# Other start addresses in on-chip memory for the operands of a decoder block's matrix products

## The chip, the cores and the metric

The kernel runs on one core of one Trainium2 chip. A core has a matrix engine (TensorE; the profile calls its products PE and its weight loads PEld), a vector engine (DVE), a scalar engine (ACT), GpSimd (POOL) and a queue that issues transfers (SP). They share an on-chip memory of 128 partitions; a tile lies at the same byte address in each partition. The metric is the device time of one execution in microseconds (us). Before the change three runs gave 1021.38, 1021.69 and 1025.06 us; the median is 1021.69 us.

## The reference

One decoder layer on 512 tokens of width 1024, all in 32-bit floats:

```python
u = modulate(rmsnorm(h, g_norm_ffn1[l]), sh1, sc1)
h = h + 0.5 * gt1 * swiglu(u, w_ffn1_in[l], w_ffn1_out[l])
u = modulate(rmsnorm(h, g_norm_mix[l]), sh2, sc2)
h = h + gt2 * token_mixing(u, cos, sin, w_in[l], ...)
u = modulate(rmsnorm(h, g_norm_ffn2[l]), sh3, sc3)
h = h + 0.5 * gt3 * swiglu(u, w_ffn2_in[l], w_ffn2_out[l])
return rmsnorm(h, g_final)
```

`swiglu` multiplies u (512 by 1024) with a 1024 by 5632 matrix, combines the halves as silu(a) * b, and multiplies by a 2816 by 1024 matrix. `token_mixing` projects u to 4608 columns, runs a causal pooling mixer and a dilated window attention over parts of them, gates both and projects back to 1024. The nine vectors of shift, scale and gate come from a 1024 by 9216 product with the condition vector.

## The kernel before, in words

**Split operands.** Every large product uses the 4-byte type float32r, and every operand is held as a rounded part ("hi") and a remainder ("lo"). One product is three matmuls (`mm3`, L323 to L325): hi weights with hi activations, hi weights with lo activations, lo weights with hi activations. In each, 128 by 128 weights are loaded into the array (the stationary operand) and the activations stream past them (the moving operand), 512 or 256 columns of tokens at a time. The trace has a weight load for every matmul, and it runs while the matmul before it streams.

**The ring of weights.** Weights come from memory in chunks, mostly 1024 columns wide (4096 bytes per partition), through three raw buffers. ACT writes the hi part into `whi` (L280), DVE the lo part into `wlo` (L292). Both are rings of `RING` = 7168 columns, that is seven chunks; `plan` lists all chunks in the order of use, and `room` (L235) gives each chunk the next place in the ring, in units of 128 columns (256 or 512 for three kinds of chunk in the mixing). A unit that does not fit before the end of the ring starts again at its beginning, so a chunk may be written in two pieces, which is one more instruction on ACT and one more on DVE. The splitting runs three or four chunks ahead of TensorE.

**Activations.** `UH` and `UL` hold u of the current sub-layer (eight tiles of 512 tokens), `HI` and `HK` the hi and lo parts of silu(a) * b, `MH` and `ML` those of the gated merge, `SH0..2` and `SL0..2` three sums of blocks of u.

**Three kinds of rows of products.** (1) Products with 512 columns: the first pairs of an FFN (`ffn_pair`; in the first FFN four pairs at once in `startup`, L1482 to L1486), the tiles of the mixing, and the output products of the FFN on `HI`/`HK`. (2) `duo` (L714): two pairs of an FFN's hidden tiles as seven block products in place of eight, each one chunk and 24 matmuls of 256 columns (`product`, L703; matmuls at L710, L711, L712). The fourth sum is a part of u itself; product 2 of a duo uses the sum `SH0`/`SL0`, product 3 `S1`, product 5 `S2`, the four others u. There are 16 duos, in eight rows; between two rows stand four chunks of output products (96 matmuls of 512 columns). (3) The ends of the three sub-layers and the beginning of the next (`out_tail`, `out_end`, `head`): products done first for tokens 0 to 255 and then for 256 to 511, so with 256 columns. Four of the mixing's value products also stream 256 columns, with the roles of weights and u exchanged (L1209 to L1211).

**Where the operands lie.** The tiles are laid out one after the other from address 1152, so that their start modulo 256 bytes is fixed by the sizes of those before. A tile of 128, 256 or 512 columns takes a multiple of 512 bytes, so all matmuls on one tile see the same remainder. In the built program:

| operand | before: start modulo 256 bytes |
|---|---|
| all weights in `whi` and `wlo` | 128 |
| `UH`, `UL` in both FFNs | 64 |
| `UH`, `UL` in the mixing (`place_u` moves them by 16 columns) | 128 |
| sum 0 | 128 |
| sums 1 and 2 (a pad of 192 bytes, `padb`, stands in front) | 64 |
| `HI`, `HK`, `MH`, `ML` and the other operands of the mixing | 128 |

TensorE works through its instructions in the order written; nothing is scheduled automatically.

Of the kernel before, what the change touches and what calls it, by code (L numbers as in the profile page):

```python
# [8 lines left out]
F32 = mybir.dt.float32  # L9
F32R = mybir.dt.float32r  # L10
# [4 lines left out]
P = 128  # L15
T = 512
HT = 256
D = 1024
KT = 8
# [91 lines left out]


FIRST = 4
RING = 7 * 1024


U_AT = (0, 16, 0)

PLAIN = {0: 8, 2: 4}
PARTS = ((0, 4), (4, 8), (8, 12), (12, 16), (16, 22))  # L120
# [3 lines left out]
def pairs_before(n, part):  # L124

    k1 = PARTS[part][1]
    return k1 if part + 1 == len(PARTS) or (n == 2 and part == 0) else k1 + 2


def chunk_widths():  # L130
    outs = [D] * (KT // 2 * (len(PARTS) - 1)) + [(FT - PARTS[-1][0]) * P] * KT
    f1 = [2 * FIRST * P] * KT + [D] * (2 * (FT - FIRST)), outs
    mix = [D] * 20 + [D, D] + [D, D, 4 * P] * (KT - 1) + [4 * P] + [D] * KT
    return f1, mix, ([D] * (2 * FT), outs)


class Kernel:
# [6 lines left out]
    def plan(self):  # L144
        (i1, o1), mix, (i2, o2) = chunk_widths()
        self.chunks = []
        for name, ws in (("wf1i", i1), ("wf1o", o1), ("wmix", mix), ("wf2i", i2), ("wf2o", o2)):
            off, rec = 0, []
            for w in ws:
                rec.append((name, off, w))  # L150
                off += P * w
            self.chunks.append(rec)
        f1i, f1o, mx, f2i, f2o = self.chunks


        self.loads, self.order, self.last = [], [], {}

        def plain(recs):
            for r in recs:
                n = len(self.loads)  # L160
                self.loads.append(r)
                self.last[n] = len(self.order)
                self.order.append((r[2], n, ("raw", n), None))

        def blocks(recs):
            n = len(self.loads)
            self.loads.extend(recs)
            r11, r12, r22, r21 = (("raw", n + i) for i in range(4))
            x0, x1 = ("x", 0), ("x", 1)
            for need, src, make in ((0, r11, None), (1, x0, (x0, r12, r11)), (2, x1, (x1, r22, x0)), (3, r21, None),  # L170
                                    (3, r12, (r12, r22, r12)), (3, r22, None), (3, x0, (x0, r21, x1))):
                for j, x in enumerate((r11, r12, r22, r21)):
                    if x == src or (make and x in make):
                        self.last[n + j] = len(self.order)
                self.order.append((D, n + need, src, make))

        def ffn(n, ins, outs, first):
            j, at = first, 0
            if first:
                plain(ins[:KT])  # L180
                at = KT
            for part, (k0, k1) in enumerate(PARTS):
                while j < pairs_before(n, part):
                    if j < PLAIN[n]:
                        plain(ins[at:at + 2])
                        j, at = j + 1, at + 2
                    else:
                        blocks(ins[at:at + 4])
                        j, at = j + 2, at + 4
                plain(outs[part * KT // 2:(part + 1) * KT // 2] if part + 1 < len(PARTS) else outs[-KT:])  # L190

        ffn(0, f1i, f1o, FIRST)
        base = len(self.order)
        plain(mx)
        ffn(2, f2i, f2o, 0)
        self.fetched = self.done = self.made = 0
        self.pos, self.held, self.retired, self.half = 0, None, [], None
        self.at, self.start, self.top = {}, {}, 0
        self.buf = {}
        self.units = {base + i: 2 * P for i in (4, 5)}  # L200
        self.units.update({base + i: T for i in range(16, 20)})
# [33 lines left out]
    def room(self, i, held):  # L235


        w, u, at, pieces = self.order[i][0], self.unit(i), self.top, []
        for c in range(0, w, u):
            if at % RING + u > RING:  # L240
                at += RING - at % RING
            o = at % RING
            if pieces and pieces[-1][0] + pieces[-1][1].stop - pieces[-1][1].start == o:
                pieces[-1] = (pieces[-1][0], slice(pieces[-1][1].start, c + u))
            else:
                pieces.append((o, slice(c, c + u)))
            at += u
        low = min((self.start[j] for j in range(held, i)), default=self.top)
        return (pieces, at) if at - low <= RING else None

# [201 lines left out]
        self.nc.vector.scalar_tensor_tensor(self.UL[k][:, hs], t[:, hs], S, self.UH[k][:, hs],  # L452
                                            op0=OP.add, op1=OP.subtract)

    def place_u(self, n):
        self.UHv, self.ULv = (x[:, U_AT[n]:U_AT[n] + KT * T] for x in (self.UHall, self.ULall))
        self.UH, self.UL = ([x[:, k * T:(k + 1) * T] for k in range(KT)] for x in (self.UHv, self.ULv))

    def norm_steps(self, n, hs):

        t, done = {}, [0]

        def upto(k):
            while done[0] <= min(k, KT - 1):
                i = done[0]
                if i == 0:
                    t[0] = self.norm_a(n, 0, hs)
                if i + 1 < KT:
                    t[i + 1] = self.norm_a(n, i + 1, hs)
                self.norm_b(n, i, hs, t.pop(i))  # L470
                done[0] += 1
        return upto
# [9 lines left out]
    def out_tail(self, ms, ksrc, gate, nxt, squares):  # L482


        nc = self.nc
        tiles, starts = {}, {}
        A, Bh = slice(0, HT), slice(HT, T)
        step = None
        self.held = self.pos
        for h, hs in enumerate((A, Bh)):  # L490
            for m in ms:
                bank = self.nb()
                if h == 0:
                    starts[m] = self.pos
                    tiles[m] = ksrc(m)
                    starts[m + 1] = self.pos
                if h == 0 and m == ms[0]:
                    nc.scalar.preload_act_table(AF.Sqrt)
                if self.done < self.pos + 4:
                    self.split_hi()  # L500
                ks = tiles[m]
                for i, (hi, lo, uh, ul) in enumerate(ks):
                    if h == 1 and m == ms[1] and i == 3:
                        self.stats_t(self.B[6], A)
                    if h == 1 and m == ms[2] and i == 1:
                        self.spread(self.B[6], A)
                        self.place_u(nxt)
                        step = self.norm_steps(nxt, A)
                        step(0)
                    self.mm3(bank[:, hs], hi, lo, uh[:, hs], ul[:, hs], i == 0, i == len(ks) - 1)  # L510
                s = squares(m)[:, :HT]
                self.tail_step(m, hs, bank, gate, s)
                if h == 1:
                    self.held = starts[m + 1]
                    if step:
                        step(1 if m != ms[-1] else 3)
                self.split_lo()
                nc.vector.tensor_tensor(self.acc[:, hs], self.acc[:, hs], s, op=OP.add)
                self.fetch()
        self.stepA = step  # L520
# [171 lines left out]
    def step(self):  # L692

        self.now += 1
        due = [f for t, f in self.put if t <= self.now]
        self.put = [x for x in self.put if x[0] > self.now]
        for f in due:
            f()
# [105 lines left out]
    def open_sums(self):  # L804
        st = ExitStack()
        bp = st.enter_context(self.tc.tile_pool(name="fs", bufs=1))
        self.S = []
        for i in range(3):
            self.S.append([bp.tile([P, 4 * HT], F32R, name=f"S{x}{i}") for x in "HL"])
            if i == 0:  # L810
                bp.tile([P, 48], F32, name="padb")
        self.S.append([x.rearrange("p (k t) -> p k t", k=KT)[:, :4, HT:] for x in (self.UHv, self.ULv)])
        return st

# [520 lines left out]
    def build(self):  # L1335
# [6 lines left out]
        tl = lambda n, w, dt=F32: per.tile([P, w], dt, name=n)  # L1342
        self.free = [tl(f"raw{i}", CW) for i in range(3)]

        self.hi, self.lo = tl("whi", RING, F32R), tl("wlo", RING, F32R)
        self.vecs = tl("vecs", 106)
        self.H = [tl(f"H{k}", T) for k in range(KT)]
        self.UHall = tl("UH", KT * T + 16, F32R)
        cst, self.eps = tl("cst", 163), tl("eps", 1)
        self.ULall = tl("UL", KT * T + 16, F32R)  # L1350
        self.place_u(0)
        self.AR = tl("AR", 2 * T)
        self.acc, self.R = self.AR[:, :T], self.AR[:, T:]
        self.mod, self.part = tl("mod", 72), tl("part", 1)
# [197 lines left out]
```

## Time and profile before

| | |
|---|---|
| median of the three runs | 1021.69 us |
| the profiled execution: its own time / its span | 1025.08 / 1023.3 us |
| PE busy, matmul records | 1012.1 us, 6364 |
| PEld busy | 914.9 us |
| DVE / ACT / POOL busy | 753.2 / 434.8 / 26.0 us |
| granted TensorE clock over the span | 0.998 |

A matmul's row has a start and a duration. Durations overlap, because the next matmul starts before the last results of the one before are out; what a matmul costs is the distance from its start to the next start. The prediction calls this the pitch, and reads it from the view of instructions in order of time, over a stretch of equal matmuls: time between two starts, divided by the matmuls between them.

### The profile page before, as it was taken

What the parts mean: (1) busy time and instruction counts of PE and PEld (TensorE: products, weight loads), DVE (VectorE), ACT (ScalarE), POOL (GpSimd) and SP (SyncE); (2) the same over time, 40 slices, a digit from 0 to 9 for tenths busy, and PEclk for the clock granted to TensorE, in tenths of its full rate; (3) what the DMA queues carried; (4) which work ended last, traced back from release to release, by engine and by line L of the source; (5) the groups of instructions that cost most, each with busy time, mean ns of one, the idle gap of its engine ahead of it and who ended that gap; (6) DMA issues with size and microseconds to landing.
All of it is one profiled execution on the core that took longest, in us unless ns stands there. A gap on an engine that the chain in (4) does not pass through costs nothing.

```text
span 1023.3 us, 15508 instructions
## 1 busy us (share of the span) xinstructions
PE 1012.1 (99%) x6364; PEld 914.9 (89%) x6364; DVE 753.2 (74%) x1082; ACT 434.8 (42%) x638; POOL 26.0 (3%) x30
## 2 busy tenths in 40 slices
PE   8999999999999999999999999999999999999997
PEld 7888898989999899889988888998899899998997
DVE  6969879889786777779446776577787776676754
ACT  5453352534445552334314333454365354352552
POOL 0000000000000000006100000000000000000001
PEclk9999999999999999999999999999999999999999
DMA  8856365555533513222154774322244234241312
GB/s 315 285 177 256 112 238 162 172 162 188 165 115 106 157 35 103 62 83 83 32 185 156 268 263 127 104 63 72 94 155 135 83 103 145 84 144 45 112 32 83
DMA packets 43113, 139.60 MB, mean 136 GB/s; under 512 B 4897, under 2 KB 8225, under 8 KB 43042
## 3 DMA queue, kind: packets, MB, share of 16 engines
q1 hardware_dynamic: 42354, 137.95, 41.3%
q8 instruction: 50, 0.82, 0.3%
q10 hardware_dynamic: 688, 0.66, 0.2%
q14 instruction: 21, 0.17, 0.1%
HBM read 135.82 MB, written 2.77 MB: 135 GB/s over the span
## 4 chain that ended last, share of the span: by engine, by line
PE 95%; DVE 3%; DMA 1%; ACT 0%; issue 0%; DVEq 0%; ACTq 0%
PE bank L323 17%; PE bank L324 17%; PE bank L325 17%; PE bank L710 10%; PE bank L712 10%; PE bank L711 10%; PE bank L1486 1%; PE bank L1484 1%; PE bank L1482 1%; PE bank L1080 1%; PE bank L1259 1%; PE bank L1411 1%; PE bank L1260 1%; PE bank L1261 1%; PE bank L1028 1%; PE bank L1057 1%
## 5 line engine op out<-in xcount | busy, mean ns | idle before, releaser
L292 DVE TENSOR_TENSOR wlo<-raw,whi 128x1024 fp32r<-128x1024 f32 (+2 forms) x151 | 175.5, 1165 | 69.0 <-ACT whi L280 68.8
L280 ACT ACTIVATE whi<-raw 128x1024 fp32r<-128x1024 f32 (+2 forms) x151 | 150.4, 1003 | 42.6 <-DVE raw L228 39.8
L323 PE MATMUL bank<-UH,whi 128*128 128x512 f32 (+1 forms) x432 | 159.0, 368 | 0.0
L324 PE MATMUL bank<-UL,whi 128*128 128x512 f32 (+1 forms) x432 | 154.9, 359 | 0.2 <-DVE UL L452 0.2
L325 PE MATMUL bank<-UH,wlo 128*128 128x512 f32 (+1 forms) x432 | 154.9, 359 | 0.0
L323 PE MATMUL bank<-HI,whi 128*128 128x512 f32 (+1 forms) x406 | 146.8, 362 | 0.0
L324 PE MATMUL bank<-HK,whi 128*128 128x512 f32 (+1 forms) x406 | 146.5, 361 | 0.0
L325 PE MATMUL bank<-HI,wlo 128*128 128x512 f32 (+1 forms) x406 | 146.5, 361 | 0.0
L710 PE MATMUL bank<-UH,whi 128*128 128x256 f32 x512 | 141.6, 277 | 0.0
L711 PE MATMUL bank<-UL,whi 128*128 128x256 f32 x512 | 141.6, 277 | 0.0
L712 PE MATMUL bank<-UH,wlo 128*128 128x256 f32 x512 | 141.6, 277 | 0.0
L292 DVE TENSOR_TENSOR wlo<-X,whi 128x1024 fp32r<-128x1024 f32 (+2 forms) x88 | 104.4, 1188 | 39.5 <-ACT whi L280 39.3
L710 PE MATMUL bank<-SH,whi 128*128 128x256 f32 x384 | 107.1, 279 | 0.3 <-ACT u L717 0.3
L711 PE MATMUL bank<-SL,whi 128*128 128x256 f32 x384 | 106.9, 278 | 0.0
L712 PE MATMUL bank<-SH,wlo 128*128 128x256 f32 x384 | 106.9, 278 | 0.0
L280 ACT ACTIVATE whi<-X 128x1024 fp32r<-128x1024 f32 (+2 forms) x88 | 89.3, 1028 | 33.1 <-DVE X L228 32.1
L711 PEld LDWEIGHTS bank<-UL,whi 128*128 128x128 f32 x512 | 96.1, 188 | 0.3
L710 PEld LDWEIGHTS bank<-UH,whi 128*128 128x128 f32 x512 | 96.1, 188 | 0.3
L712 PEld LDWEIGHTS bank<-UH,wlo 128*128 128x128 f32 x512 | 96.4, 188 | 0.0
L325 PEld LDWEIGHTS bank<-UH,wlo 128*128 128x128 f32 x432 | 81.3, 188 | 12.8
L324 PEld LDWEIGHTS bank<-UL,whi 128*128 128x128 f32 x432 | 81.5, 189 | 12.3 <-issue 0.5
L323 PEld LDWEIGHTS bank<-UH,whi 128*128 128x128 f32 x432 | 81.4, 189 | 11.9 <-issue 0.5
(225 smaller groups left out, 1748.5 us busy)
## 6 DMA issues: line engine op xcount, KB each, us to landing
ada<-wada SPq DMA_DIRECT2D x47, 512.0 KB, 5.0
raw<-wmix SPq DMA_DIRECT2D x44, 512.0 KB, 3.9
raw<-wf1i SPq DMA_DIRECT2D x34, 512.0 KB, 4.5
raw<-wf2i SPq DMA_DIRECT2D x30, 512.0 KB, 3.6
X<-wf2i SPq DMA_DIRECT2D x14, 512.0 KB, 3.5
cs<-wada SPq DMA_DIRECT2D x12, 512.0 KB, 3.5
AR<-wada SPq DMA_DIRECT2D x12, 512.0 KB, 3.9
raw<-wf2o SPq DMA_DIRECT2D x12, 512.0 KB, 3.6
```

The costliest lines, as they stand in the source:

```text
L280: self.nc.scalar.activation(self.hi[:, y], r[:, x], AF.Copy)
L292: self.nc.vector.tensor_tensor(self.lo[:, y], r[:, x], self.hi[:, y], op=OP.subtract)
L323: M(ps, hi, uh, start=start, stop=False)
L324: M(ps, hi, ul, start=False, stop=False)
L325: M(ps, lo, uh, start=False, stop=stop)
L710: M(o, hi, uh, start=start and p == 0 and k == 0, stop=False, skip_group_check=True)
L711: M(o, hi, ul, start=False, stop=False, skip_group_check=True)
L712: M(o, lo, uh, start=False, stop=k == 3, skip_group_check=True)
L1028: M(S[:, o + i * P:o + i * P + P], qz[:, (2 * i + h) * P:(2 * i + h + 1) * P], k[:, toks], start=True, stop=True)
L1057: nc.tensor.transpose(b[:, i * P:i * P + P], p[:, i * P:i * P + P], self.ident)
L1080: M(o, pt[:, blk * P:blk * P + P], v, start=i == 0, stop=i == len(srcs) - 1)
L1259: M(b, self.UH[k][:, c::4], hi, start=k == 0, stop=False)
```

## The change

`UH` and `UL` get a pad of 16 columns (64 bytes) in front and a fixed place; `place_u` and the pad `padb` go. u and all sums then start at 128 modulo 256 bytes in all sub-layers. A chunk of weights may be marked as shifted: it then starts at 16 columns after a multiple of 64 columns in the ring, which is 192 modulo 256 bytes; others stay at 128. Marked are the chunks of all 256-column products on u, sums, `HI` and `MH` (not the value products with exchanged roles), and the one chunk of 512-column products in front of each row of such chunks. The ring grows from 7168 to 7296 columns. All tiles behind it move by 1024 bytes, which leaves their remainder as it was.

```diff
-RING = 7 * 1024
-U_AT = (0, 16, 0)
+RING = 7 * 1024 + 128
+SHIFT = 16
...
     def blocks(recs):
         n = len(self.loads)
+        self.shifted.update(range(len(self.order) - 1, len(self.order) + 7))
...
+    def shift(i):
+        self.shifted.update(range(len(self.order) - i, len(self.order)))
...
                     if j < PLAIN[n]:
                         plain(ins[at:at + 2])
+                        if n and j < 2:
+                            shift(2)
...
         ffn(0, f1i, f1o, FIRST)
+        shift(5)
         base = len(self.order)
         plain(mx)
+        self.shifted.update(range(base, base + 4))
+        shift(4)
         ffn(2, f2i, f2o, 0)
+        shift(6)
...
         w, u, at, pieces = self.order[i][0], self.unit(i), self.top, []
+        shift = SHIFT if i in self.shifted else 0
+        at += (shift - at) % 64
         for c in range(0, w, u):
             if at % RING + u > RING:
-                at += RING - at % RING
+                at += RING - at % RING + shift
...
-    def place_u(self, n):
-        self.UHv, self.ULv = (x[:, U_AT[n]:U_AT[n] + KT * T] for x in (self.UHall, self.ULall))
...
-            if i == 0:
-                bp.tile([P, 48], F32, name="padb")
...
-        self.UHall = tl("UH", KT * T + 16, F32R)
+        tl("pad0", 16)
+        self.UHv = tl("UH", KT * T, F32R)
         cst, self.eps = tl("cst", 163), tl("eps", 1)
-        self.ULall = tl("UL", KT * T + 16, F32R)
-        self.place_u(0)
+        tl("pad1", 16)
+        self.ULv = tl("UL", KT * T, F32R)
```

In the built programs the instructions of every engine stand in the same order before and after, except that 30 more chunks are written to the ring in two pieces: 30 more instructions at L280 on ACT and 30 more at L292 on DVE. The float32r matmuls by the remainders of weights (w) and moving operand (u):

| columns | before | after | matmuls |
|---|---|---|---|
| 256 | w 128, u 64 | w 192, u 128 | 2496 |
| 256 | w 128, u 128 | w 192, u 128 | 1044 (384 of them on sum 0) |
| 512 | w 128, u 64 | w 128, u 128 | 456 |
| 512 | w 128, u 128 | w 192, u 128 | 228 (chunks in front of rows) |
| 512 | w 128, u 64 | w 192, u 128 | 24 (chunk in front of the first row) |
| 512 | w 128, u 128 | unchanged | 1530 |
| both | value products with exchanged roles | unchanged | 168 |

More of the change, by code (lines that the diff above doesn't have):

```diff
@@ L156, in plan @@
         self.loads, self.order, self.last = [], [], {}
+        self.shifted = set()
         def plain(recs):
@@ L453, in norm_b @@
                                             op0=OP.add, op1=OP.subtract)
-    def place_u(self, n):
-        self.UHv, self.ULv = (x[:, U_AT[n]:U_AT[n] + KT * T] for x in (self.UHall, self.ULall))
-        self.UH, self.UL = ([x[:, k * T:(k + 1) * T] for k in range(KT)] for x in (self.UHv, self.ULv))
     def norm_steps(self, n, hs):
@@ L506, in out_tail @@
                         self.spread(self.B[6], A)
-                        self.place_u(nxt)
                         step = self.norm_steps(nxt, A)
@@ L1347, in build @@
         self.H = [tl(f"H{k}", T) for k in range(KT)]
-        self.UHall = tl("UH", KT * T + 16, F32R)
+        tl("pad0", 16)
+        self.UHv = tl("UH", KT * T, F32R)
         cst, self.eps = tl("cst", 163), tl("eps", 1)
-        self.ULall = tl("UL", KT * T + 16, F32R)
-        self.place_u(0)
+        tl("pad1", 16)
+        self.ULv = tl("UL", KT * T, F32R)
+        self.UH, self.UL = ([x[:, k * T:(k + 1) * T] for k in range(KT)] for x in (self.UHv, self.ULv))
         self.AR = tl("AR", 2 * T)
```

## The prediction

> **What bounds the kernel now.** I read the page first (busy times, then the chain that ended last, then the costliest groups), and after it TensorE's instructions in order of time, where the starts show what one matmul costs. The first fence is the page.
>
> ```profile
> PE 1012.1 (99%) x6364; PEld 914.9 (89%) x6364; DVE 753.2 (74%) x1082; ACT 434.8 (42%) x638; POOL 26.0 (3%) x30
> PE 95%; DVE 3%; DMA 1%; ACT 0%; issue 0%; DVEq 0%; ACTq 0%
> L710 PE MATMUL bank<-UH,whi 128*128 128x256 f32 x512 | 141.6, 277 | 0.0
> ```
>
> TensorE is busy 99% of the span and carries 95% of the chain; the large groups have no idle time before them (last column). In the view of waits TensorE waits 3.3 us in the start-up and 1.1 us in four places after it. So nothing but the pitch of the matmuls sets the end, and a pitch changed by p ns on n matmuls moves the end by n times p.
>
> The next fence is the view in order of time (start in us, duration, engine, line). It holds the first row of five stretches of equal matmuls, and each time the row that follows the stretch.
>
> ```profile
> 108.87 0.39 PE L323 MATMUL bank<-UH,whi 128*128 128x512 f32 x1
> ...
> 131.27 0.28 PE L710 MATMUL bank<-UH,whi 128*128 128x256 f32 x1
> ...
> 134.00 0.28 PE L710 MATMUL bank<-SH,whi 128*128 128x256 f32 x1
> ...
> 136.86 0.29 PE L710 MATMUL bank<-SH,whi 128*128 128x256 f32 x1
> ...
> 150.48 0.39 PE L323 MATMUL bank<-HI,whi 128*128 128x512 f32 x1
> ...
> 172.26 0.28 PE L710 MATMUL bank<-UH,whi 128*128 128x256 f32 x1
> ...
> 175.09 0.28 PE L710 MATMUL bank<-SH,whi 128*128 128x256 f32 x1
> ...
> 177.96 0.29 PE L710 MATMUL bank<-SH,whi 128*128 128x256 f32 x1
> ```
>
> All weights start at 128, so only the moving operand differs. Pitches:
> - 512 columns, u at 64 (108.87 to 131.27, four chunks of 24): 22.40 us / 96 = 233.3 ns.
> - 512 columns, `HI` at 128 (150.48 to 172.26): 21.78 / 96 = 226.9 ns.
> - 256 columns, u and sums 1, 2 at 64 (136.86 to 150.48, five products): 13.62 / 120 = 113.5 ns; single matmuls alternate 113, 113, 114, so 113.3 settled.
> - 256 columns, sum 0 at 128 (134.00 to 136.86 and 175.09 to 177.96): 119.2 and 119.6 ns. The 256-column ends on `HI` and `MH` at 128 run at 119.9 in the same view.
> - 256 columns, u at 64, but right behind a row of 512 columns at 128 (172.26 to 175.09): 2.83 / 24 = 117.9 ns, to the end of the product. Behind a row of 512 columns at 64 (131.27 to 134.00) it is 113.8. So there are two settled pitches at the same addresses, and what ran before picks one.
>
> The start address is thus worth 6.4 ns a matmul, with opposite signs: 512 columns want 128 against 128, 256 columns want 64 bytes between weights and u.
>
> **The change part by part.** It goes by the profiled execution, 1025.08 us (span 1023.3), 3.4 us above the median of the runs; each saving is taken off the median too.
>
> (1) *512-column products on u in the FFNs go to 128/128*: 456 matmuls from 233.3 to 226.9: 456 x 6.4 = **-2.9 us**. The class is in the trace. 192 of them are the start-up, where vector work could take over as the bound: there a chunk costs DVE 5.32 us (first norm operations of two chunks, 22.97 and 28.29) and TensorE 24 x 233.3 = 5.60; at 226.9 it is 5.45, still the longer. The gain stays.
>
> (2) *256-column products at 128/128 get 64 bytes between the operands*: 1044. Sum 0: 16 products x 24 x (119.4 - 113.3) = 2.3 us, and the product behind each, which settles at 114.1, 0.3 us. The ends of sub-layers: 660 x (119.9 - 113.3) = 4.3 us, less some 0.3 where the statistics stand between them and the second pitch comes up for about 20 matmuls each time (66 x 4.5 ns). Together **-6.6 us**, if the new pair of addresses is as fast as the old one.
>
> (3) *Entry to the rows*: seven of the eight rows of duos now begin at 117.9. The chunk in front now has 192/128, which should leave the state that the 64-bytes-apart row leaves before 131.27. 7 x 24 x 4.5 = **-0.8 us**.
>
> (4) *The chunks in front*: 228 matmuls of 512 columns lose 128/128: 228 x 6.4 = **+1.5 us**.
>
> (5) *The other 256-column products*, 2496 from 128/64 to 192/128: no row of before has weights of this type at 192. Here lies the unknown. Nearest rows: 113.3 (the same 64 bytes apart, weights ahead), 117.9 (the same, other settled pitch), 119.9 (the same u). Below: the matmuls of the attention, whose weights alone set their pace (L1028), start 111 to 112 ns apart; 1.5 ns below 113.3 would be 5.3 us over all 3540. Above: 119.9 costs 2303 x 6.6 + 193 x 2.2 = 15.6 us. I take 113.3, **0 us**, since u alone cannot explain the rows: 128 is bad for 256 columns and good for 512, so it is the two streams against each other, and their distance is kept. That a weight load might be slower from 192 has rows of its own, in the views of lines 1080 and 1028 (weights at 192 and at 128; ns, least/median/most):
>
> ```profile
> L1080 PEld LDWEIGHTS bank<-v,probT x120: 187/192/193, 416.7 to 517.4; 128*128 128x128 f32 x120
> L1028 PEld LDWEIGHTS bank<-k,qz x64: 187/192/192, 470.7 to 502.9; 128*128 128x128 f32 x64
> ```
>
> They are the same.
>
> (6) *30 more pieces on ACT and DVE.* DVE takes 1224 ns for 1024 columns and 688 for 512, so 152 ns fixed; ACT 1050 and 624, so 198. That is 4.6 and 5.9 us in all, hidden by TensorE: DVE is busy 178.5 of 217.0 us in the stretch 131 to 348, 197.7 of 273.0 in 717 to 990. From the end of a chunk's L292 row to the first matmul that reads it the trace has at least 2.5 us, over ten times a piece. If that cover went, 30 x 0.35 = 10 us would be the most. Transfers and their order stay; a raw buffer comes free at most 0.35 us later. Moving the tiles costs nothing: all other remainders are kept.
>
> Sum: -2.9 - 6.6 - 0.8 + 1.5 = **-8.8 us**: 1016.3 for the profiled execution, **1012.9** for the median.
>
> **The rivals.**
>
> *A, slower: the rows settle at the second pitch, 117.9.* Place: the entry of each row of 256 columns. Today it ends after one product because sum 0 at 128 breaks it; afterwards nothing in the row does, so it would hold for whole rows. Price: 2303 x 4.6 = +10.6, 1044 x (117.9 - 119.9) = -2.1, and (1) and (4): +7.1, so 1028.8. It decides when over about 55% of the 3540 matmuls settle there (8.8 of 16.3 us). For it: the 172.26 row; also that 192/128 with 512 columns has never been seen. Against it: the entry at 131.27.
>
> *B, slower: not the distance counts, but u alone (or weights at 192 are worse).* Then (5) costs 15.6, (2) and (3) bring nothing, (4) costs nothing, (1) stays: +12.7, so 1034.4. Against it: the opposite signs, and the equal loads.
>
> *C, between: some rows settle well and some don't*, or only part (1) and a part of (2) arrive: 1016 to 1025.
>
> *D, the addresses do nothing*, the two streams reading independently, so that only hidden pieces are added: 1021.7. Against it: 113.5 and 119.2 on the same line with the same weights. The Trainium skill ("TensorE: Matmul & The Clock Gate", Part 2, what happens when you issue a matmul) states this independence: two read ports, so that loading the next weights takes nothing from the running matmul. By it the sum would be 0; the trace disagrees, by 6 ns a matmul.
>
> **How the numbers follow.** Forecast 0.68, its own range 1010 to 1016 (below, a pitch nearer 112 for part of the matmuls; above, the tails' and entries' terms lost). A 0.12, B 0.08, C 0.10, D 0.02. The range 1009 to 1024 holds the forecast and nearly all of C and D, and leaves out A and B. About 0.5%, 5.1 us, is what a measurement of this kernel can tell from no change. Faster is the forecast and a little of C; same is the rest of C, and D; slower is A and B.
>
> **What would show it.** The same view, in every row of duos: products of 24 matmuls 2.72 us apart, sum 0 among them (2.86 now), the first of a row 2.73 in place of 2.83; start-up chunks of eight banks 5.45 apart; the chunk in front 24 x 233 = 5.60. The durations at L710 would be 276 ns throughout (278 mean on the sums now). I am wrong by A if whole rows show 2.83, by B if 2.86 or more; if DVE waits appear before L711 or L712, (6) has failed.

## The result, and the profile after

The changed kernel takes 1026.12 us (median of 14 runs), the kernel before 1022.62 us in as many (the 1021.69 us above is the median of the first three of them): 1.0031 times as long, 95% interval 1.0022 to 1.0040. The forecast was 1012.9, the range 1009 to 1024. It is 3.5 us slower, not 8.8 us faster. The page of the changed kernel:

```profile
PE 1013.7 (99%) x6364; PEld 917.7 (90%) x6364; DVE 756.2 (74%) x1112; ACT 437.7 (43%) x668; POOL 26.3 (3%) x30
PE 96%; DVE 2%; DMA 1%; ACT 0%; issue 0%; SPq 0%; DVEq 0%; ACTq 0%
L719 PE MATMUL bank<-UH,whi 128*128 128x256 f32 x512 | 143.6, 281 | 0.0
```

TensorE is the bound as before, with no idle time in front of the groups. The 30 more pieces on ACT and DVE (668 and 1112 instructions) hold nothing up. What moved is the third line: the 256-column matmuls on u last 281 ns in the mean, 277 before. 281 is the duration of the matmuls that ran at the second pitch, 117.8 ns, in the kernel before; those at 113.3 last 276, those at equal remainders 283.

The view in order of time of the changed kernel shows the entry to the first row of duos, and a whole product stretch of the second row, each line there the first matmul of a product:

```profile
126.10 0.39 PE L337 MATMUL bank<-UH,whi 128*128 128x512 f32 x1
126.33 0.40 PE L338 MATMUL bank<-UL,whi 128*128 128x512 f32 x1
126.57 0.39 PE L339 MATMUL bank<-UH,wlo 128*128 128x512 f32 x1
126.80 0.28 PE L719 MATMUL bank<-UH,whi 128*128 128x256 f32 x1
126.92 0.28 PE L720 MATMUL bank<-UL,whi 128*128 128x256 f32 x1
...
168.53 0.28 PE L719 MATMUL bank<-UH,whi 128*128 128x256 f32 x1
...
171.36 0.28 PE L719 MATMUL bank<-SH,whi 128*128 128x256 f32 x1
...
174.19 0.28 PE L719 MATMUL bank<-SH,whi 128*128 128x256 f32 x1
...
177.01 0.28 PE L719 MATMUL bank<-UH,whi 128*128 128x256 f32 x1
...
179.84 0.28 PE L719 MATMUL bank<-SH,whi 128*128 128x256 f32 x1
```

Products follow each other every 2.83 us, 117.8 ns a matmul, sum 0 among them. All eight rows begin so, and seven stay so to their end. The third row shows that nothing in the addresses forbids the better pitch: there a matmul comes 27 ns late, and from then on the row runs at 113.3.

```profile
241.24 0.28 PE L721 MATMUL bank<-UH,wlo 128*128 128x256 f32 x1
241.36 0.31 PE L719 MATMUL bank<-SH,whi 128*128 128x256 f32 x1
241.51 0.28 PE L720 MATMUL bank<-SL,whi 128*128 128x256 f32 x1
241.63 0.28 PE L721 MATMUL bank<-SH,wlo 128*128 128x256 f32 x1
...
242.08 0.28 PE L719 MATMUL bank<-SH,whi 128*128 128x256 f32 x1
242.20 0.28 PE L720 MATMUL bank<-SL,whi 128*128 128x256 f32 x1
```

Added up over the two traces by class (time from each matmul's start to the next):

| class | matmuls | before, us | after, us | change |
|---|---|---|---|---|
| 512 columns on u in the FFNs, to 128/128 | 456 | 106.5 | 103.5 | -3.0 |
| chunks in front of rows, to 192/128 | 252 | 57.3 | 58.8 | +1.5 |
| duos, products on sum 0 | 384 | 45.9 | 45.1 | -0.7 |
| duos, all others | 2304 | 262.8 | 270.4 | +7.7 |
| ends and beginnings of the sub-layers, 256 columns | 852 | 102.3 | 100.4 | -1.9 |
| other float32r matmuls | 1698 | 383.4 | 383.4 | 0.1 |

The sum is +3.7 us. Two terms of it change from profile to profile, and here they cancel. In the third row of the kernel before, a wait near 244 us makes one start 469 ns late and the next 109, which is 0.6 us of the 262.8; after, the start there is 27 ns late, and in the other profiles up to 336 ns in all. And the beginning of the second FFN takes 23.2 us after, but 22.6 to 22.7 in the ten other profiles of this study.

The stretch from the first float32r matmul to the start of the last matmul is 996.4 us before and 1000.1 after. I use this stretch below, beside the medians, since what lies ahead of it differs from execution to execution: the first float32r matmul starts between 16.4 and 19.9 us in the eleven profiled executions.

### The profile page after: what moved, and what is told of

Read it like the earlier page. It is cut to its first block, busy times and chain, and to the rows that moved or that the text cites. A ratio compares the mean times of both kernels' runs of the same rounds, so it can differ in the third digit from the quotient of the medians.

```text
span 1024.9 us, 15581 instructions
## 1 busy us (share of the span) xinstructions
PE 1013.7 (99%) x6364; PEld 917.7 (90%) x6364; DVE 756.2 (74%) x1112; ACT 437.7 (43%) x668; POOL 26.3 (3%) x30
## 4 chain that ended last, share of the span: by engine, by line
PE 96%; DVE 2%; DMA 1%; ACT 0%; issue 0%; SPq 0%; DVEq 0%; ACTq 0%
PE bank L337 18%; PE bank L338 18%; PE bank L339 18%; PE bank L721 10%; PE bank L719 10%; PE bank L720 10%; PE bank L1491 1%; PE bank L1495 1%; PE bank L1493 1%; PE bank L1087 1%; PE bank L1266 1%; PE bank L1267 1%; PE bank L1268 1%; PE bank L1035 1%; PE bank L1064 1%; DMA H<-xT 1%
## 5 line engine op out<-in xcount | busy, mean ns | idle before, releaser
L306 DVE TENSOR_TENSOR wlo<-raw,whi 128x1024 fp32r<-128x1024 f32 (+6 forms) x173 | 177.4, 1037 | 70.6 <-ACT whi L294 70.4
L294 ACT ACTIVATE whi<-raw 128x1024 fp32r<-128x1024 f32 (+6 forms) x173 | 152.5, 900 | 41.6 <-DVE raw L240 38.9
L306 DVE TENSOR_TENSOR wlo<-X,whi 128x1024 fp32r<-128x1024 f32 (+4 forms) x96 | 105.3, 1103 | 43.2 <-ACT whi L294 42.8
L294 ACT ACTIVATE whi<-X 128x1024 fp32r<-128x1024 f32 (+4 forms) x96 | 89.9, 957 | 32.2 <-DVE X L240 31.3
```

Of the source, the lines that this page charges most:

```text
L294: self.nc.scalar.activation(self.hi[:, y], r[:, x], AF.Copy)
L306: self.nc.vector.tensor_tensor(self.lo[:, y], r[:, x], self.hi[:, y], op=OP.subtract)
```

## The experiments

A pair like 192/128 gives the remainders of the weights and of the streamed operand. T1 is the theory after the result: at 64 bytes apart a 256-column matmul has two settled pitches, 113.3 and 117.8, at either pair of addresses, and what ran before picks one; a product with equal remainders throws a row to 113.3. T2 is rival B of the prediction: the pair 192/128 is itself slower. Times stand against the kernel before on the same chip.

**e1: sum 0 at 192.** In the changed kernel,

```diff
         for i in range(3):
+            if i < 2:
+                bp.tile([P, 48 if i else 16], F32, name=f"pads{i}")
             self.S.append([bp.tile([P, 4 * HT], F32R, name=f"S{x}{i}") for x in "HL"])
```

> Edit: the changed kernel with sum 0 (SH0, SL0) moved to 192, so that product 2 of every duo runs with weights and sum at the same remainder (192/192); all else as after. Theory T1 (two settled pitches, history picks one): the 256-column matmuls at 64 bytes apart can run at 113.3 or 117.8 ns; a product with both operands at the same remainder, as sum 0 was before the change, throws them into the 113.3 state. Then every product behind the first product on sum 0 of a row runs at 113.3: 88 products x 24 x 4.5 = 9.5 us, less 1.0 us for the nine products that already run so after the change, less 16 x 24 x 1.5 = 0.6 us for sum 0 at 119.3: about -7.9 us against after, 1018.2. Theory T2 (192/128 itself is the slower pair than 128/64): the rows stay at 117.8, sum 0 costs 0.6 more: 1026.7.

Measured: 1018.07 us, 0.9957 times before (0.9944 to 0.9971); stretch 992.3. The second row in order of time, first matmul of each product:

```profile
166.77 0.28 PE L719 MATMUL bank<-UH,whi 128*128 128x256 f32 x1
...
169.59 0.28 PE L719 MATMUL bank<-SH,whi 128*128 128x256 f32 x1
...
172.47 0.28 PE L719 MATMUL bank<-SH,whi 128*128 128x256 f32 x1
...
175.21 0.28 PE L719 MATMUL bank<-UH,whi 128*128 128x256 f32 x1
...
177.93 0.28 PE L719 MATMUL bank<-SH,whi 128*128 128x256 f32 x1
...
180.65 0.28 PE L719 MATMUL bank<-UH,whi 128*128 128x256 f32 x1
```

2.82 us for the first product, 2.88 for sum 0 at 192/192, 2.74 behind it and then 2.72, that is 113.3 ns at 192/128. T2 falls: the new pair is as fast as the old one.

**e2: sum 0 at 64 in the kernel before.** The opposite test, without any move of weights:

```diff
+            if i == 0:
+                bp.tile([P, 48], F32, name="padb")
             self.S.append([bp.tile([P, 4 * HT], F32R, name=f"S{x}{i}") for x in "HL"])
-            if i == 0:
-                bp.tile([P, 48], F32, name="padb")
```

> Edit: the kernel before, with the 192-byte pad moved in front of sum 0, so that all three sums lie at 64; weights stay at 128, nothing else changes. T1: nothing breaks the second pitch any more, so rows that begin at 117.8 (seven of eight, those behind output products at 128/128) stay there; the first row stays at 113.3. 83 products x 24 x 4.5 = +9.0 us, sum 0 at 117.8 in place of 119.4 -0.7: about +8.2 us against before, 1030.8, or 1.3 less where a wait throws a row over. T2: sum 0 goes from 119.4 to 113.3, -2.6 us: 1020.0.

Measured: 1029.70 us, 1.0073 times before (1.0051 to 1.0095); stretch 1003.7. The second row, the same kind of lines:

```profile
171.90 0.28 PE L710 MATMUL bank<-UH,whi 128*128 128x256 f32 x1
...
174.73 0.28 PE L710 MATMUL bank<-SH,whi 128*128 128x256 f32 x1
...
177.56 0.28 PE L710 MATMUL bank<-SH,whi 128*128 128x256 f32 x1
...
180.38 0.28 PE L710 MATMUL bank<-UH,whi 128*128 128x256 f32 x1
```

2.83 us each, to the end of the row; the first row alone runs at 113.3 throughout. So in the kernel before the "slow" address of sum 0 was what kept the rows fast: with the sum moved, its own products are 0.7 us cheaper (45.9 to 45.1 us by the classes above) and the other products of the duos 8.1 us dearer (262.8 to 270.9).

**e3: no shift of the chunk in front.**

```diff
-            self.shifted.update(range(len(self.order) - 1, len(self.order) + 7))
+            self.shifted.update(range(len(self.order), len(self.order) + 7))
...
-        shift(5)
+        shift(4)
...
-        shift(4)
+        shift(3)
...
-        shift(6)
+        shift(5)
```

> Edit: the changed kernel without the shift of the one chunk of 512-column products in front of each row (it stays at 128/128); the rows as after. T1 and T2 both: front chunks at 226.9 in place of 233.3, 228 x 6.4 = -1.5 us, rows still at 117.8: 1024.6. If the front chunk did anything for the entry, the rows would now begin at another pitch than 117.8; if it had helped, above 1024.6.

Measured: 1023.87 us, 1.0018 times before (1.0008 to 1.0028); stretch 998.2, 1.9 less than after. Rows begin at 117.8 as with the shift. The shift of the chunk in front only costs: 1.7 of the 1.9 us are these chunks themselves.

**e4: the first chunk of a row at 128/128 as well.**

```diff
+            row = self.order and self.order[-1][3] is not None
-            self.shifted.update(range(len(self.order) - 1, len(self.order) + 7))
+            self.shifted.update(range(len(self.order) + (0 if row else 1), len(self.order) + 7))
...
-        shift(5)
+        shift(3)
...
-        shift(4)
+        shift(2)
...
-        shift(6)
+        shift(4)
```

> Edit: the changed kernel, but neither the chunk in front of a row nor the first chunk of the row is shifted: the row begins with one product at 128/128 and goes on at 192/128. T1: that first product (119.7) throws the rest of the row to 113.3: 104 products x 24 x 4.5 = -11.2 us, less 1.0 for those that are there already, +0.4 for the first products, -1.5 for the front chunks, about -1.3 in the ends of the sub-layers: -12.6 us against after, 1013.5, and 9 us below before. T2: the rows stay at 117.8: +0.4 - 1.5, 1025.0.

Measured: 1025.57 us, 1.0029 times before (1.0012 to 1.0046); stretch 998.6. A miss for T1: the first product ran at 119.6, and the rest of the row at 117.8 (only the third row went to 113.3, behind two late starts in its middle). Equal remainders alone do not do it. What differs from e1 is the way back to 64 apart: here the weights move from 128 to 192, there the streamed operand moves from 192 to 128. T1' is T1 with this condition, and e8 and e9 test it.

**e5: e1 without the shift in front**, the edit of e3 on e1.

> Edit: run e1 (sum 0 at 192) without the shift of the chunk in front of a row. If the products on sum 0 alone set the state of a row: rows as in e1 (first product 117.8, sum 0 about 120, the rest 113.3) and 228 front matmuls at 226.9 in place of 233.3, -1.5 us: 1016.6. If the front chunk was needed for it: rows at 117.8, about 1024.

Measured: 1016.91 us, 0.9937 times before (0.9920 to 0.9954); stretch 990.9. As expected: the products on sum 0 set the state, the chunk in front is not needed. It is the fastest median of the study, 0.6% below the kernel before.

**e6: equal remainders once per row.** On e5,

```diff
+            if self.order[-1][3] is not None:
+                self.twice.add(len(self.order) + 1)
             self.shifted.update(range(len(self.order), len(self.order) + 7))
...
-        shift = SHIFT if i in self.shifted else 0
+        shift = 2 * SHIFT if i in self.twice else SHIFT if i in self.shifted else 0
```

> Edit: run e5, but from the second duo of a row on the weights of the product on sum 0 lie at 0 modulo 256, so that they are 64 bytes apart from sum 0 (0/192) like the others; only the first duo of a row has the product with equal remainders. If the distance alone counts and a state once set lasts: 8 products on sum 0 at 113.3 in place of 119.2, -1.1 us, and 0.15 us behind them: 1015.3 if e5 is 1016.6. If the two changes of place at the ends of that product throw the row to the second pitch: up to 56 products x 24 x 4.5 = +6.0 us: 1022.

Measured: 1018.38 us (1015.93 to 1019.57), 0.9949 times before (0.9931 to 0.9967); stretch 990.7, 0.2 below e5. Neither case came fully: the later products on sum 0, at 0/192, ran at 117.6, and those behind them at 113.3 again. That saves 8 x 24 x 1.6 = 0.3 us by the pitches, against 1.1 expected; by the medians there is no gain over e5.

**e7: part (1) alone, at another place.** In the kernel before the weights of the 512-column products on u in the FFNs go to 64, so 64/64:

```diff
-RING = 7 * 1024
+RING = 7 * 1024 + 128
...
+                self.moved.update(range(len(self.order) - KT, len(self.order)))
...
+                        if n == 0 or j > 1:
+                            self.moved.update(range(len(self.order) - 2, len(self.order)))
...
+        shift = 48 if i in self.moved else 0
+        at += (shift - at) % 64
...
-                at += RING - at % RING
+                at += RING - at % RING + shift
```

> Edit: the kernel before, with one change alone: the weights of the 512-column products on u in the FFNs lie at 64 (ring 7296 columns), so that these 480 matmuls run at 64/64 in place of 128/64. If the distance between the operands counts: 226.9 in place of 233.3, 480 x 6.4 = -3.1 us, +0.1 for the first row, which now begins at 117.8: 1019.4. If the place itself counts (128 is good, 64 is not): no gain, 1022.4.

Measured: 1019.73 us, 0.9963 times before (0.9950 to 0.9976); stretch 993.3, 3.0 less. 226.7 ns at 64/64: for 512 columns it is the distance that counts, not the place.

**e8: equal remainders on sum 0 by the weights.** In the changed kernel,

```diff
             self.shifted.update(range(len(self.order) - 1, len(self.order) + 7))
+            self.shifted.discard(len(self.order) + 1)
```

> Edit: the changed kernel, in which the chunk of weights for the product on sum 0 is not shifted: that product runs at 128/128 as in the kernel before, and like e1 has equal remainders at the same place of every row, but it is entered and left by moving the weights, where e1 (and the kernel before) moves the streamed operand. T1 as it stood (equal remainders throw the row to 113.3): as e1, 1018.1. T1', after e4 missed (it matters that the streamed operand is what changes): rows stay at 117.8, sum 0 costs 0.6: 1026.7.

Measured: 1028.59 us, 1.0051 times before (1.0031 to 1.0070); stretch 1001.3. The second row, first matmul of each product:

```profile
170.56 0.28 PE L720 MATMUL bank<-UH,whi 128*128 128x256 f32 x1
...
173.39 0.28 PE L720 MATMUL bank<-SH,whi 128*128 128x256 f32 x1
...
176.27 0.28 PE L720 MATMUL bank<-SH,whi 128*128 128x256 f32 x1
...
179.09 0.28 PE L720 MATMUL bank<-UH,whi 128*128 128x256 f32 x1
...
181.92 0.28 PE L720 MATMUL bank<-SH,whi 128*128 128x256 f32 x1
```

2.88 us at equal remainders as in e1, but 2.82 and 2.83 behind it, where e1 has 2.74 and 2.72. The same product, at the same place of the row, with equal remainders: left by a move of the streamed operand it throws the row to 113.3, left by a move of the weights it does not. That the equal pair is 192/192 in e1 and 128/128 here is not the reason: the kernel before has 128/128 too, leaves it by a move of the streamed operand, and goes to 113.3. T1' holds here, T1 as it stood falls. The median lies above both cases. The stretch is 1.2 us above after: sum 0 costs 0.9, the third row, in which nothing comes late here, stays at 117.8 and costs 1.0, and the beginning of the second FFN gives 0.6 back.

**e9: the entry of before, reached by the weights.** e7, but the chunk in front of the first row stays at 128/64:

```diff
-                            self.moved.update(range(len(self.order) - 2, len(self.order)))
+                            self.moved.update(range(len(self.order) - 2, len(self.order) - (n == 0 and j == 7)))
```

> Edit: run e7 (before, with the weights of the 512-column products on u in the FFNs at 64, so 64/64), except for the one chunk in front of the first row of duos, whose weights stay at 128: 72 matmuls at 64/64, then 24 at 128/64, then the row at 128/64. These are the addresses of the kernel before at the entry of that row, but the 64 bytes of distance are reached by a move of the weights, as in the changed kernel, and not of the streamed operand. If the way in decides (T1'): the front chunk alternates 231 and 236 ns as in the changed kernel, and the first product of the row runs at 117.8. If the addresses decide (128/64 against 192/128): the front chunk runs at 233 and 234 and the first product at 113.8, as in the kernel before. In time the two differ by 0.1 us, so only the trace tells.

Measured: 1022.59 us in a single run, the kernel before 1023.85 in a single run on the same chip; one run each tells nothing at this size. The end of the chunk in front and the start of the row, first in the kernel before, then in e9 (128/64 in both):

```profile
130.57 0.39 PE L323 MATMUL bank<-UH,whi 128*128 128x512 f32 x1
130.81 0.39 PE L324 MATMUL bank<-UL,whi 128*128 128x512 f32 x1
131.04 0.39 PE L325 MATMUL bank<-UH,wlo 128*128 128x512 f32 x1
131.27 0.28 PE L710 MATMUL bank<-UH,whi 128*128 128x256 f32 x1
131.39 0.28 PE L711 MATMUL bank<-UL,whi 128*128 128x256 f32 x1
131.51 0.28 PE L712 MATMUL bank<-UH,wlo 128*128 128x256 f32 x1
```

```profile
127.87 0.39 PE L330 MATMUL bank<-UL,whi 128*128 128x512 f32 x1
128.10 0.40 PE L331 MATMUL bank<-UH,wlo 128*128 128x512 f32 x1
128.33 0.39 PE L329 MATMUL bank<-UH,whi 128*128 128x512 f32 x1
128.56 0.40 PE L330 MATMUL bank<-UL,whi 128*128 128x512 f32 x1
128.80 0.39 PE L331 MATMUL bank<-UH,wlo 128*128 128x512 f32 x1
129.03 0.28 PE L716 MATMUL bank<-UH,whi 128*128 128x256 f32 x1
```

The distances that follow are the traces' own, in ns; the views round them. Before, the chunk in front runs at 233, 234, 233, 233 with one duration, 0.39, and the row settles at 113.3 within three matmuls. In e9 durations of 0.39 and 0.40 alternate, the starts are 231 and 236 apart, and the first product takes 117.8, as in the changed kernel. At the same remainders the way in decides; 512 columns at 64 apart have two states too, of the same mean, and these lead to different pitches in the row behind.

## Why the prediction was wrong

- **Step (1), -2.9 us: right.** -3.0 in the trace, and the stretch of e7, which makes this change alone (for 480 matmuls), is 3.0 shorter; the start-up kept its gain.
- **Step (4), +1.5: right in size** (+1.5 in the trace; e3 gets 1.7 back on these chunks).
- **Step (5), 0 us: this failed, with (3).** Step (5) took the lower of the two settled pitches, 113.3, for all 2496 matmuls; the duos without sum 0 cost +7.7 us. Its reason was sound, that the distance is kept (e1: 113.3 at 192/128), but the distance does not settle the pitch.
- **Step (3), -0.8: the wrong inference that fed (5).** It held that a chunk in front at 64 apart leaves the state seen before 131.27. The prediction read the pitch of that chunk, 233.3, and not its single starts; these show 233 and 234 there, against 231 and 236 in the chunk that the changed kernel has. e9 shows that the two are different states, and that the second leads to 117.8. The trace of before could have told that there are two: its start-up, and the chunks from 695.23 us, also at 128/64, have 231 and 236.
- **Step (2), -6.6: mostly lost.** Sum 0 brought -0.7 in place of -2.3, as it ran at 117.5 in the mean instead of 113.3. The 660 matmuls at the ends and beginnings of the sub-layers brought -2.5 of 4.3: only the beginning of the mixing reached 113.3 nearly throughout (178 of 192 matmuls, 23.2 to 22.0 us), most of the ends run at 117.8. The table has -1.9 for their class, since the 192 at the beginning of the second FFN, which step (5) had at no change, fell back from 113.3 to 117.8 in this execution (22.6 to 23.2 us). And sum 0 at equal remainders was no loss to be removed but what held the rows at 113.3 (e2).
- **Step (6), nothing: right.** After the first 18 us TensorE waits 0.8 us in three places, before 1.1 us in four, by the views of waits.
- **Rival A came, and its place and reason were right**: the rows settle at the second pitch at their entry, because no product on sum 0 breaks it any more. It was given 0.12. Its price, +7.1, was twice what came: the third row went to 113.3, worth 1.0 us; so did the beginning of the mixing, which brought 1.2 us where A gives 0.4; and the wait of 0.6 us in the third row of before did not come after. What makes up the rest, about 1 us, I have not taken apart. Rival B falls with e1, D with e2 and e7; the rule of the Trainium skill named there ("TensorE: Matmul & The Clock Gate", Part 2) says that loading the next weights takes no read bandwidth from the running matmul. This case's traces speak against it: with the same instructions, the pitch depends on where the weights and the streamed operand lie against each other (113.3, 117.8 and 120.0 ns for 256 columns).

What stays open is why. The rule "moved by the streamed operand: 113.3" does not cover every entry: behind 512-column products at 128/128 the row of the kernel before is entered by a move of the streamed operand, and begins at 117.8; there the number of columns changes at the same matmul. All moves of one operand out of equal remainders were of two kinds, the weights 64 bytes up or the streamed operand 64 bytes down; the opposite directions were not tried, nor were distances of 128 or 192 bytes, so that 256 bytes is the whole period is not shown. That two reads of the on-chip memory meet in the same part of it is a likely cause, but no run shows it.

Late matmuls are a second way to change the state, and an uncertain one. Ten of the eleven profiles have late starts at the same place of the third row (in e8 nothing comes late). They threw the row from 117.8 to 113.3 in three (after, e3, e4), from 113.3 to 117.8 in two (e7, e9), and left it as it was in five. The third row after was therefore luck, not a gain of the change.

## What to carry to other kernels

When a kernel is bound by back-to-back matmuls, read the single starts, not only the mean pitch of a class: a class can have several settled pitches at the same addresses, and the matmuls before pick one. Before a product that looks slow is "repaired", ask what it does to those behind it; here the repair of 384 matmuls cost 2304 others 3.3 ns each, and keeping them slow while taking the other gains (e5) made the kernel 0.6% faster than before. A change of addresses is tested best by moving one operand at a time, since moving the weights and moving the streamed operand to the same distance gave different pitches.

## What the runs showed of the hardware

- The start address modulo 256 bytes of the two operands changes a float32r matmul's pitch: 512 columns 226.7 to 226.9 ns at equal remainders (128/128, 64/64) and 233.3 at 64 bytes apart; 256 columns 119.2 to 120.0 at equal remainders (128/128, 192/192) and 113.3 or 117.8 at 64 bytes apart (128/64, 192/128).
- At 64 bytes apart both lengths have two states that last: 113.3 and 117.8 ns for 256 columns (113.3 over 216 matmuls in a row, 117.8 over up to 504); 233/234 and 231/236 for 512.
- Which state a stream takes depends on what ran before: after a product of 256 columns at equal remainders it is 113.3 when the streamed operand moves (e1, 114.1 to 114.2 in the first product) and 117.8 when the weights move (e4, e8).
- One matmul that came 27 ns late changed the state for the rest of a row; in e7 and e9 late starts changed it the other way, and in five profiles not at all.
